# A threshold search on ScalarE: the next candidate worked out by ScalarE's own small instructions in place of GpSimd's

## The chip, the cores and the metric

The kernel runs on one core of a Trainium2 chip. The core has five engines that run at the same time, each with its own queue that is worked through strictly in order: TensorE (PE in the tables; PEld is its loading of weights), VectorE (DVE), ScalarE (ACT), GpSimd (POOL) and SyncE (SP, which issues the DMAs). They wait for each other by semaphores. The metric is the device time of one execution in microseconds (us).

## The reference

One decoder layer on 1024 tokens of width 1024, all in float32. A conditioning vector gives shift, scale and gate rows; `h = x * (1 + scale1) + shift1`; one projection gives q, k, v, the indexer's `iq`, `ik`, `iw`, and `u`. The mixer is sparse attention beside a causal pooling of `u`; then come a LayerNorm, a SwiGLU block of width 2816 and a second LayerNorm. The part that the change touches is the choice of the 256 keys that a query may attend to:

```
score = einsum('bqh,bqhs->bqs', w, relu(logits))
score = where(causal, score, -inf)
_, idx = top_k(score, 256)          # per query, of up to 1024 keys
s = softmax(q k^T over the keys in idx)
```

## The kernel before

Queries stand in eight tiles of 128, one query per partition. A query of tiles 0 and 1 has at most 256 keys, so all of them are taken. For tiles 2 to 7 the kernel looks, for every query, for the 256th largest score and turns the score row into a mask that is added in the attention (line 1058). A score is a float32 whose upper and lower 16 bits are searched one after the other, bit by bit: 15 passes over the upper half, then 16 over the lower one. A pass compares a row of 16-bit keys with a candidate per partition, counts, and moves the candidate up or down by half the last step.

Tiles 7, 6 and 5 are searched by VectorE (`search_v`). Tiles 4 and 3 together, and tile 2 alone, are two searches on ScalarE (`search_a`, line 686; `TILES_A`, line 37). Here a pass over one tile is one `Sign` activation of the keys with the negated candidate as the bias column; its accumulator adds the signs of a row into the column `cntc`. The instruction shows in the trace as ACTIVATE `junkA_T<-keys_T` (tile 4, 640 columns), `junkA_T<-keysA_X` (tile 3, 512) or `junkB_X<-keysA_X` (tile 2, 384), followed by an ACTIVATION_READ_ACCUMULATOR. Then GpSimd works out the next candidate in four instructions on columns of 1 or 2 elements per partition (lines 701 to 704; tile `colsA_X`): the sum less a limit, compared and scaled, shifted, added to the candidate. The next pass waits for them. Below, a step of the pair search is one pass over tiles 4 and 3 with its update, and a step of the single search is one pass over tile 2. There are 31 of each.

What runs around the searches: until 170 us the scores are computed (TensorE's `lg`, ScalarE's `relu_K`, VectorE's sums into `score_X`). Then come the projections of `u`, `k` and `v`: their weights are split into a high and a low part (`ws_W`; high by ScalarE, low by VectorE or GpSimd), `u` is copied to `ub_V`, summed over windows by VectorE and GpSimd, split into `phi_V` and `plo_V`, and its result leaves as `pout_K`; `k` goes to `rope_V` and `kr_K`, `v` to `vf_V`. From 395 us on the attention runs over units of one pair of heads and one query tile, tiles 7 and 6 first: the query's operands `qab_H` and `qab_W`, the scores `s`, VectorE's maximum (CUSTOM_DVE `sm_H<-s,score_X`), ScalarE's exponential, GpSimd's division, transposes `pT`, products `o`. After it come the output projection and the SwiGLU block, to 1336 us.

The order in each queue is not written out by hand. Line 154 records each instruction, estimates when its engine would reach it, and before issuing it asks `fill` (line 772) whether a step of an open search fits in front: a search says what it needs next by `yield`, an engine's letter and an estimated time. So the search steps are spread as filling between the other work by an estimate made when the program is built; on the chip the queues then run in that fixed order (`PIN`, line 39). `need(i)` (line 768) makes the attention's first use of a tile wait until its search is in the queues.

A ScalarE search has two places where VectorE takes part: after the 15th step (lines 706 to 718: the upper half is fixed, the keys are rewritten for the lower half), and after the 31st (lines 720 to 743: the mask, with a scan over the row for ties).

Of the kernel before, what the change touches and what calls it, by code (L numbers as in the profile page):

```python
# [20 lines left out]
P = 128  # L21
# [31 lines left out]
SYNC = 0.06  # L53
UPDATE = "G"
POOL_AT = 3
# [126 lines left out]
def decoder_layer_kernel(  # L182
# [458 lines left out]
    def bisect(tiles, cols, on_act):  # L641
# [23 lines left out]
        for m, i in enumerate(tiles):  # L665
# [4 lines left out]
            if on_act:  # L670
                V.tensor_scalar(one(thr, m), one(kp, m), -2.0, -float(P * (i + 1)), ALU.mult, ALU.add)
        sum_w = sum(w_(i) for i in tiles)
# [13 lines left out]
        def search_a(bits, low):  # L686

            V.memset(cand, 0.5 - float(1 << (bits - 1)))
            for b in range(bits - 1, -1, -1):
                yield "A", 1.13 * sum_w + 0.18 * nt  # L690
                for m, i in enumerate(tiles):
                    A.activation(trash(i), kv[i].bitcast(U16 if low else I16), AF.Sign, bias=one(cand, m),
                                 accum_out=one(cntc, m))
                yield UPDATE, 0.5
                half = float(1 << (b - 1)) if b > 0 else 1.0
                if UPDATE == "V":
                    V.tensor_tensor(pr, cntc, thr, ALU.is_ge)
                    V.tensor_scalar(pr, pr, -float(1 << b), half, ALU.mult, ALU.add)
                    V.tensor_tensor(cand, cand, pr, ALU.add)
                else:  # L700
                    G.tensor_tensor(pr, cntc, thr, ALU.subtract)
                    G.tensor_scalar(pr, pr, 0.0, -float(1 << b), ALU.is_ge, ALU.mult)
                    G.tensor_scalar(pr, pr, half, 0.0, ALU.add, ALU.add)
                    G.tensor_tensor(cand, cand, pr, ALU.add)
            yield "V", 0.1
            V.tensor_scalar(cand, cand, -1.0, 0.5, ALU.mult, ALU.add)

        yield from (search_a(15, False) if on_act else search_v(15, kp, False))
        V.tensor_copy(M, cand)
        for m, i in enumerate(tiles):  # L710
# [5 lines left out]
            if on_act:  # L716
                V.tensor_scalar(one(thr, m), one(ng, m), -2.0, -float(P * (i + 1)), ALU.mult, ALU.add)
        yield from (search_a(16, True) if on_act else search_v(16, ng, True))
# [53 lines left out]
    def fill(q, until):  # L772
        while True:
            todo = [st for st in streams if (st[1][0] == q.name and start(st) + st[1][1] <= until + SLACK.get(q.name, 0.0))
                    or (st[1][0] == "G" and start(st) < until)]
            if not todo:
# [1130 lines left out]
```

## Time and profile before

| | us |
|---|---|
| median of 3 runs | 1338.66 (1336.64 to 1338.84) |
| profiled execution, its own time | 1337.45 |
| its span in the trace | 1335.70 |
| PE busy in the span | 1197.2 (90%) |
| DVE busy | 1071.7 (80%) |
| POOL busy | 780.7 (58%) |
| ACT busy | 604.0 (45%) |

The span is the time from the first to the last instruction in the trace; the profiled execution's time lies 1.75 us above it, and 1.21 us below the median. The busy shares are averages over stages with different limits; the stage in which the searches run is 143 to 433 us. In a timeline row, the number in brackets at the end is how long the engine sat idle before the instruction, and behind the arrow stands what ended the wait.

### The profile page before, as it was taken

Reading aid. Unit: us, or ns where it says so; the run is one execution under the profiler, and the core shown is the slowest. Engines: PE = TensorE matmul, PEld = TensorE weight load, DVE = VectorE, ACT = ScalarE, POOL = GpSimd, SP = SyncE. Lnnn points to the kernel's source line nnn. Section 1 sums busy time; section 2 is a strip of 40 time slices with the busy share of each in tenths; the row PEclk is TensorE's granted clock in tenths of the full one; section 3 lists DMA queues with packets and bytes.
Section 4 is the critical chain, followed back from the end, with each engine's and each line's share of the span. In section 5 each row is a group of like instructions: output and inputs, shape, how many; then the busy total and the mean of one; then the engine's idle time right before and its main releaser. Section 6 shows DMA issues by size and latency. Waiting matters only on the chain.

```text
span 1335.7 us, 16132 instructions
## 1 busy us (share of the span) xinstructions
PE 1197.2 (90%) x5462; PEld 932.9 (70%) x5462; DVE 1071.7 (80%) x1769; ACT 604.0 (45%) x1149; POOL 780.7 (58%) x743
## 2 busy tenths in 40 slices
PE   7979996967768997999789999999999999999996
PEld 6646575746545664788677878878787887878775
DVE  6898889899997688566688687777768787777698
ACT  3346642653746776625644333333334243333431
POOL 1392684766434354527678484755748485666848
PEclk8989997978878998999799999999999999999998
DMA  9640030301000166430030201112120101113113
GB/s 337 232 158 17 17 95 16 111 32 48 32 24 1 33 213 223 156 119 1 24 102 27 78 32 64 36 60 67 44 79 32 64 32 64 63 36 122 39 62 122
DMA packets 34905, 103.91 MB, mean 78 GB/s; under 512 B 3843, under 2 KB 3843, under 8 KB 33286
## 3 DMA queue, kind: packets, MB, share of 16 engines
q1 hardware_dynamic: 34822, 102.88, 22.2%
q8 instruction: 43, 0.70, 0.2%
q14 instruction: 40, 0.33, 0.1%
HBM read 93.42 MB, written 9.45 MB: 77 GB/s over the span
## 4 chain that ended last, share of the span: by engine, by line
PE 38%; DVE 6%; POOL 4%; issue 2%; ACT 1%; DVEq 0%; POOLq 0%; ACTq 0%
PE gu L169 24%; PE dn L169 14%; DVE act_W L169 2%; POOL wraw_R L169 1%; DVE utmp_X L169 1%; POOL wraw_W L169 1%; DVE gtmp_V L169 1%; POOL wblk_T L169 0%; DVE wblk_T L169 0%; DVE hr_H L169 0%; POOL hr_H L169 0%; DVE res_X L169 0%; DVE stat_C L169 0%; POOL wblk_V L169 0%; DVE wblk_V L169 0%
## 5 line engine op out<-in xcount | busy, mean ns | idle before, releaser
L169 PE MATMUL gu<-hr_H,wblk_V 128*128 128x512 f32 (+1 forms) x924 | 215.2, 384 | 3.7 <-POOL wblk_V L169 1.9
L169 PE MATMUL gu<-hr_H,wblk_T 128*128 128x512 f32 (+1 forms) x924 | 215.8, 385 | 2.9 <-POOL wblk_T L169 1.9
L169 PEld LDWEIGHTS gu<-hr_H,wblk_T 128*128 128x128 f32 x924 | 170.9, 189 | 39.1 <-POOL wblk_T L169 3.6
L169 PEld LDWEIGHTS gu<-hr_H,wblk_V 128*128 128x128 f32 x924 | 170.1, 188 | 40.0 <-POOL wblk_V L169 3.6
L169 DVE TENSOR_TENSOR res_X<-res_X,dn 128x512 f32<-128x512 f32 (+1 forms) x253 | 159.0, 680 | 15.4 <-PE dn L169 15.3
L169 PE MATMUL pj<-ws_W,hT_H 128*128 128x512 f32 x456 | 123.8, 420 | 17.9 <-ACT pout_K L169 5.4
L169 POOL TENSOR_TENSOR wraw_R<-wraw_R 128x512 f32<-128x512 f32 x64 | 94.3, 1479 | 47.0 <-DVE wblk_T L169 23.7
L169 POOL TENSOR_TENSOR wraw_W<-wraw_W 128x512 f32<-128x512 f32 x60 | 86.6, 1450 | 58.0 <-DVE wblk_V L169 29.3
L169 PEld LDWEIGHTS pj<-ws_W,hT_H 128*128 128x128 f32 x456 | 88.5, 200 | 45.4 <-issue 14.8
L169 POOL TENSOR_SCALAR sm_H<-sm_H,stat_X 128x1024 f32<-128x1024 f32 (+7 forms) x64 | 58.5, 927 | 70.5 <-DVE stat_X L169 53.8
L169 PE MATMUL dn<-wblk_T,act_W 128*128 128x512 f32 x324 | 79.6, 395 | 4.8 <-DVE act_W L169 4.8
L169 PE MATMUL dn<-wblk_V,act_W 128*128 128x512 f32 x324 | 78.5, 391 | 2.9 <-DVE act_W L169 2.5
L169 DVE TENSOR_SCALAR_CACHE_REDUCE junk_X<-keysD_T,colsD_X 128x1024 int16<-128x1024 int16 (+1 forms) x64 | 78.9, 1270 | 0.8
L169 PEld LDWEIGHTS dn<-wblk_T,act_W 128*128 128x128 f32 x324 | 60.9, 189 | 19.5 <-DVE act_W L169 6.9
L169 PEld LDWEIGHTS dn<-wblk_V,act_W 128*128 128x128 f32 x324 | 60.4, 188 | 17.4 <-DVE act_W L169 4.2
L169 ACT ACTIVATE wblk_V<-wraw_R 128x512 fp32r<-128x512 f32 x56 | 35.2, 629 | 80.6 <-POOL wraw_R L169 62.2
L169 ACT ACTIVATE wblk_V<-wraw_W 128x512 fp32r<-128x512 f32 x53 | 33.1, 627 | 75.1 <-POOL wraw_W L169 56.5
L169 ACT ACTIVATE wblk_T<-wraw_W 128x512 fp32r<-128x512 f32 x56 | 35.0, 628 | 66.6 <-POOL wraw_W L169 50.2
L169 POOL TENSOR_TENSOR colsA_X<-colsA_X 128x1 f32<-128x1 f32 (+1 forms) x124 | 33.9, 283 | 48.3 <-ACT junkA_T L169 37.9
L169 ACT ACTIVATE wblk_T<-wraw_R 128x512 fp32r<-128x512 f32 x52 | 32.5, 627 | 61.0 <-POOL wraw_R L169 45.6
L169 POOL TENSOR_TENSOR ws_W<-raw_R,ws_W 128x1024 fp32r<-128x1024 f32 x11 | 29.9, 2721 | 51.3 <-ACT ws_W L169 51.3
L169 ACT ACTIVATE sm_H<-sm_H,stat_X 128x1024 f32<-128x1024 f32 (+7 forms) x64 | 49.0, 768 | 18.5 <-DVE stat_X L169 15.5
(299 smaller groups left out, 2815.4 us busy)
## 6 DMA issues: line engine op xcount, KB each, us to landing
wm_K<-in_wma_dram SPq DMA_DIRECT2D x16, 512.0 KB, 10.2
modraw_V<-in_wmc_dram SPq DMA_DIRECT2D x16, 512.0 KB, 4.5
wraw_R<-in_wg_dram SPq DMA_DIRECT2D x6, 1024.0 KB, 4.8
wraw_R<-in_wd_dram SPq DMA_DIRECT2D x12, 512.0 KB, 3.6
wraw_W<-in_wup_dram SPq DMA_DIRECT2D x12, 512.0 KB, 3.6
modraw_V<-in_wmg_dram SPq DMA_DIRECT2D x10, 512.0 KB, 3.7
wraw_R<-in_wup_dram SPq DMA_DIRECT2D x10, 512.0 KB, 3.5
wraw_W<-in_wg_dram SPq DMA_DIRECT2D x5, 1024.0 KB, 4.8
```

Source lines behind the costliest of these rows:

```text
L169: ins_ = f(*a, **k)
```

## The change

The four GpSimd instructions go. In their place ScalarE issues two small activations per tile. The number of keys in a row is even, and the limit is now such that sum plus limit is odd, so that it is never zero: `Sign(cntc + thr)` gives +1 or -1, and an `Identity` activation adds that, times half the step, to the candidate. Both read and write one column of one element per partition. The start value and the end conversion are adapted on VectorE, with the same number of instructions. The recorder's estimate for a step changes too, the wait for GpSimd goes from the search's list of needs, and `fill` no longer looks for GpSimd steps. So the order that the recorder makes comes out another way on every engine between 140 and 450 us.

```
@@ bisect
-                V.tensor_scalar(one(thr, m), one(kp, m), -2.0, -float(P * (i + 1)), ALU.mult, ALU.add)
+                V.tensor_scalar(one(thr, m), one(kp, m), 2.0, float(P * (i + 1) + 1), ALU.mult, ALU.add)
@@ search_a
-                yield "A", 1.13 * sum_w + 0.18 * nt
+                yield "A", 1.0 * sum_w + 0.65 * nt
                 for m, i in enumerate(tiles):
                     A.activation(trash(i), kv[i].bitcast(U16 if low else I16), AF.Sign, bias=one(cand, m),
                                  accum_out=one(cntc, m))
-                yield UPDATE, 0.5
-                half = float(1 << (b - 1)) if b > 0 else 1.0
...
-                    G.tensor_tensor(pr, cntc, thr, ALU.subtract)
-                    G.tensor_scalar(pr, pr, 0.0, -float(1 << b), ALU.is_ge, ALU.mult)
-                    G.tensor_scalar(pr, pr, half, 0.0, ALU.add, ALU.add)
-                    G.tensor_tensor(cand, cand, pr, ALU.add)
+
+                for m in range(nt):
+                    A.activation(one(pr, m), one(cntc, m), AF.Sign, bias=one(thr, m))
+                for m in range(nt):
+                    A.activation(one(cand, m), one(pr, m), AF.Identity, scale=-0.5 * float(1 << b), bias=one(cand, m))
             yield "V", 0.1
-            V.tensor_scalar(cand, cand, -1.0, 0.5, ALU.mult, ALU.add)
+            V.tensor_scalar(cand, cand, -1.0, None, ALU.mult)
@@ fill
-            todo = [st for st in streams if (st[1][0] == q.name and start(st) + st[1][1] <= until + SLACK.get(q.name, 0.0))
-                    or (st[1][0] == "G" and start(st) < until)]
+            todo = [st for st in streams if st[1][0] == q.name and start(st) + st[1][1] <= until + SLACK.get(q.name, 0.0)]
```

The first place is ScalarE's queue in the projection of `u`, from the first split `phi_V` on. Before, one step of each search stands in front of the result `pout_K`:

```order
L169 ACTIVATE phi_V_1245<-ub_V_1243 128x1024
L169 ACTIVATE ub_V_1244<-pj_1387 128x512
L169 ACTIVATE ub_V_1244<-pj_1435 128x512
L169 ACTIVATE junkA_T_613,colsA_X_606<-keys_T_611,colsA_X_606 128x640
L169 ACTIVATE junkA_T_613,colsA_X_606<-keysA_X_605,colsA_X_606 128x512
L169 ACTIVATE junkB_X_614,colsA_X_606<-keysA_X_605,colsA_X_606 128x384
L169 ACTIVATE pout_K_1251<-po_1553,const_C_78 128x512
L169 ACTIVATE pout_K_1251<-po_1554,const_C_78 128x512
```

Now, in the same place of ScalarE's queue, three steps of the pair search stand there (the last two of them are shown) and one of the single search:

```order
L168 ACTIVATE junkA_T_613,colsA_X_606<-keys_T_611,colsA_X_606 128x640
L168 ACTIVATE junkA_T_613,colsA_X_606<-keysA_X_605,colsA_X_606 128x512
L168 ACTIVATE colsA_X_606<-colsA_X_606 128x1 x4
L168 ACTIVATE junkA_T_613,colsA_X_606<-keys_T_611,colsA_X_606 128x640
L168 ACTIVATE junkA_T_613,colsA_X_606<-keysA_X_605,colsA_X_606 128x512
L168 ACTIVATE colsA_X_606<-colsA_X_606 128x1 x4
L168 ACTIVATE junkB_X_614,colsA_X_606<-keysA_X_605,colsA_X_606 128x384
L168 ACTIVATE colsA_X_606<-colsA_X_606 128x1 x2
L168 ACTIVATE pout_K_1235<-po_1557,const_C_78 128x512
L168 ACTIVATE pout_K_1235<-po_1558,const_C_78 128x512
```

The pair search's steps have moved forward: seven stand ahead of this first `phi_V` (before: three), and all of its first 15 steps ahead of the last `phi_V` (before: nine).

The second place is VectorE's queue at the start of the attention. Before, the end of the single search (`junkB`, 128x384) is mixed into the end of VectorE's own search, and the operands `qab_H` follow:

```order
L169 TENSOR_TENSOR junkB_X_614<-junkB_X_614,keysA_X_605 128x384
L169 SCALAR_TENSOR_TENSOR score_X_77<-keys_T_612,colsD_X_615 128x768
L169 TENSOR_SCALAR score_X_77<-junkB_X_614 128x384
L169 TENSOR_SCALAR score_X_77<-score_X_77 128x768
L169 TENSOR_TENSOR keys_T_612<-keys_T_612,score_X_77 128x768
L169 TENSOR_TENSOR junk_X_609<-junk_X_609,keys_T_612 128x768
L169 TENSOR_SCALAR score_X_77<-junk_X_609 128x768
L169 TENSOR_TENSOR qab_H_2590<-qT_2597,qab_H_2590 64x512 x2
L169 ISA sm_H_2589,stat_X_2584<-s_2681,score_X_77 128x1024
L169 ISA stat_X_2584 128x1
L169 TENSOR_TENSOR qab_W_2591<-qT_2602,qab_W_2591 64x512 x2
```

Now, on VectorE, the first part of the end of the pair search (128x640, 128x512) stands there, and the first maximum (ISA `sm_H`) comes behind both operands:

```order
L168 TENSOR_SCALAR colsA_X_606<-colsA_X_606 128x2
L168 CAST colsA_X_606<-colsA_X_606 128x2
L168 TENSOR_TENSOR colsA_X_606<-colsA_X_606 128x2 x2
L168 TENSOR_SCALAR keys_T_611<-score_X_77,colsA_X_606 128x640
L168 TENSOR_SCALAR junkA_T_613,colsA_X_606<-score_X_77,colsA_X_606 128x640
L168 TENSOR_SCALAR keysA_X_605<-score_X_77,colsA_X_606 128x512
L168 TENSOR_SCALAR colsA_X_606<-colsA_X_606 128x1
L168 TENSOR_TENSOR qab_H_2528<-qT_2535,qab_H_2528 64x512
L168 SCALAR_TENSOR_TENSOR score_X_77<-keys_T_611,colsA_X_606 128x640
L168 TENSOR_TENSOR qab_H_2528<-qT_2535,qab_H_2528 64x512
L168 TENSOR_SCALAR score_X_77<-score_X_77 128x640
L168 TENSOR_TENSOR qab_W_2529<-qT_2540,qab_W_2529 64x512 x2
```

The end of the single search has moved behind the eighth maximum, and the rest of the pair search's end between the first maxima; before, the whole of it lay behind the eighth. From 450 us on the order of every engine is the same in both kernels, and SyncE's order of DMAs is the same throughout.

## Rows read from the trace of the kernel before

**Rows 1.** Window, its us; busy us of PE, PEld, DVE, ACT, POOL; PEclk, DMA, GB/s.
```profile
143.00:395.00 252.00, 192.15 (x761) 146.51 (x759) 234.49 (x401) 133.96 (x274) 155.40 (x298) 0.88 0.14 49
...
405.00:410.00 5.00, 5.00 (x11) 2.41 (x11) 2.54 (x5) 0.88 (x3) 2.57 (x4) 0.50 0.00 0
...
420.00:425.00 5.00, 4.08 (x30) 2.45 (x31) 4.96 (x8) 2.11 (x4) 2.74 (x3) 1.00 0.01 3
...
450.00:470.00 20.00, 19.93 (x144) 13.70 (x143) 13.96 (x33) 14.21 (x32) 7.54 (x8) 1.00 0.19 57
```
**Rows 2.** Waits between 133 and 450 us: total, times, longest.
```profile
ACT junkB_X L169 <- POOL colsA_X L169: 42.8, 10, 13.4
ACT junkA_T L169 <- POOL colsA_X L169: 23.1, 14, 5.7
```
**Rows 3.** DVE in the timeline: its waits that end at another engine's search work.
```profile
161.35 2.67 DVE L169 SCALAR_TENSOR_TENSOR score_X<-relu_K,const_C,score_X 128x1024 f32<-128x1024 f32 x2 [2.36 <-ACT relu_K L169]
...
177.79 2.63 DVE L169 TENSOR_TENSOR ws_W<-raw_R,ws_W 128x1024 fp32r<-128x1024 f32 x1 [1.17 <-ACT ws_W L169]
...
250.94 1.23 DVE L169 SCALAR_TENSOR_TENSOR ub_V<-ub_V,ub_V 128x1024 f32<-128x1024 f32 x1 [2.60 <-POOL ub_V L169]
...
257.01 0.15 DVE L169 TENSOR_SCALAR colsA_X<-colsA_X 128x1 f32<-128x1 f32 x1 [1.06 <-POOL colsA_X L169]
```
**Rows 4.** The tile of the search columns: ns min/median/max, first and last start us, forms.
```profile
L169 POOL TENSOR_TENSOR colsA_X<-colsA_X x124: 183/193/1926, 144.2 to 415.7; 128x1 f32<-128x1 f32 x62, 128x2 f32<-128x2 f32 x62
L169 POOL TENSOR_SCALAR colsA_X<-colsA_X x124: 223/243/1906, 145.4 to 415.3; 128x1 f32<-128x1 f32 x62, 128x2 f32<-128x2 f32 x62
L169 ACT ACTIVATE junkB_X<-keysA_X,colsA_X x31: 598/602/627, 143.4 to 364.5; 128x384 bf16<-128x384 uint16 x16, 128x384 bf16<-128x384 int16 x15
...
L169 ACT ACTIVATE junkA_T<-keys_T,colsA_X x31: 812/828/840, 152.3 to 409.4; 128x640 bf16<-128x640 uint16 x16, 128x640 bf16<-128x640 int16 x15
```
**Rows 5.** ACT by operation and form: busy us, mean ns, idle before.
```profile
L169 ACT ACTIVATE sm_H<-sm_H,stat_X 128x128 f32<-128x128 f32 x8 | 3.1, 391 | 0.4 <-DVE stat_X L169 0.4
...
L169 ACT ACTIVATE const_C<-const_C 128x8 f32<-128x8 f32 x1 | 0.2, 210 | 0.6 <-DVE const_C L169 0.6
```
**Rows 6.** ACT in the timeline, a step of each search in turn.
```profile
359.32 0.83 ACT L169 ACTIVATE junkA_T<-keys_T,colsA_X 128x640 bf16<-128x640 uint16 x1 [0.65 <-POOL colsA_X L169]
...
361.00 0.60 ACT L169 ACTIVATE junkB_X<-keysA_X,colsA_X 128x384 bf16<-128x384 uint16 x1
...
362.35 0.83 ACT L169 ACTIVATE junkA_T<-keys_T,colsA_X 128x640 bf16<-128x640 uint16 x1 [0.66 <-POOL colsA_X L169]
```
**Rows 7.** ACT in the timeline: the first two splits of `u`.
```profile
218.91 1.06 ACT L169 ACTIVATE phi_V<-ub_V 128x1024 fp32r<-128x1024 f32 x1 [7.43 <-DVE ub_V L169]
...
231.60 1.06 ACT L169 ACTIVATE phi_V<-ub_V 128x1024 fp32r<-128x1024 f32 x1 [7.27 <-DVE ub_V L169]
```
**Rows 8.** All engines in the timeline around the start of the attention.
```profile
383.32 0.14 DVE L169 TENSOR_SCALAR colsA_X<-colsA_X 128x1 f32<-128x1 f32 x1
...
392.61 0.33 DVE L169 TENSOR_SCALAR score_X<-junkB_X 128x384 f32<-128x384 bf16 x1
...
394.90 1.40 DVE L169 TENSOR_TENSOR qab_H<-qT,qab_H 64x512 fp32r<-64x512 f32 x2
...
396.88 1.22 DVE L169 CUSTOM_DVE_ANT_0 sm_H<-s,score_X 128x1024 f32<-128x1024 f32 x1 [0.58 <-PE s L169]
...
409.40 0.83 ACT L169 ACTIVATE junkA_T<-keys_T,colsA_X 128x640 bf16<-128x640 uint16 x1 [4.12 <-POOL colsA_X L169]
...
415.89 0.17 DVE L169 TENSOR_SCALAR colsA_X<-colsA_X 128x2 f32<-128x2 f32 x1
...
418.41 0.15 DVE L169 TENSOR_SCALAR colsA_X<-colsA_X 128x1 f32<-128x1 f32 x1
...
419.62 2.32 DVE L169 TENSOR_TENSOR_SCAN score_X<-keys_T,colsA_X 128x640 bf16<-128x640 bf16 x1
```
**Rows 9.** The candidate columns of DVE's own search, 133 to 433 us: busy us, mean ns, idle.
```profile
L169 DVE TENSOR_SCALAR colsD_X<-colsD_X 128x3 f32<-128x3 f32 (+3 forms) x41 | 12.9, 322 | 1.1
```

More of the change, by code (lines that the diff above doesn't have):

```diff
@@ L53 @@
 SYNC = 0.06
-UPDATE = "G"
 POOL_AT = 3
@@ L693, in search_a @@
                                  accum_out=one(cntc, m))
-                yield UPDATE, 0.5
-                half = float(1 << (b - 1)) if b > 0 else 1.0
[L696 to L700, printed above, removed]
-                    G.tensor_tensor(pr, cntc, thr, ALU.subtract)
-                    G.tensor_scalar(pr, pr, 0.0, -float(1 << b), ALU.is_ge, ALU.mult)
-                    G.tensor_scalar(pr, pr, half, 0.0, ALU.add, ALU.add)
-                    G.tensor_tensor(cand, cand, pr, ALU.add)
+                for m in range(nt):
+                    A.activation(one(pr, m), one(cntc, m), AF.Sign, bias=one(thr, m))
+                for m in range(nt):
+                    A.activation(one(cand, m), one(pr, m), AF.Identity, scale=-0.5 * float(1 << b), bias=one(cand, m))
             yield "V", 0.1
-            V.tensor_scalar(cand, cand, -1.0, 0.5, ALU.mult, ALU.add)
+            V.tensor_scalar(cand, cand, -1.0, None, ALU.mult)
         yield from (search_a(15, False) if on_act else search_v(15, kp, False))
@@ L716, in bisect @@
             if on_act:
-                V.tensor_scalar(one(thr, m), one(ng, m), -2.0, -float(P * (i + 1)), ALU.mult, ALU.add)
+                V.tensor_scalar(one(thr, m), one(ng, m), 2.0, float(P * (i + 1) + 1), ALU.mult, ALU.add)
         yield from (search_a(16, True) if on_act else search_v(16, ng, True))
```

## The prediction

> **What bounds the kernel now.** I read the busy times by window first, then the waits, then the search's own tile, then the timeline of ScalarE and VectorE stretch by stretch. From 143 to 395 us VectorE is busy 234.49 of 252 us, ScalarE 133.96, GpSimd 155.40, TensorE 192.15 [rows 1]: this stage ends when VectorE is through with its own search of tiles 7, 6 and 5, since the attention begins with those tiles. So what ScalarE or GpSimd save counts here only where VectorE stands and waits for them. At the start of the attention TensorE is full at a granted clock of 0.50, which is its lower level of 1.2 GHz (405 to 410 us, 5.00 of 5); then VectorE is the full one (420 to 425: 4.96, TensorE 4.08); from 450 us TensorE is (19.93 of 20) [rows 1]. All later work is in the same order in both kernels, so that what is gained or lost by 450 us is handed on to the end.
>
> ScalarE's searches spend much time on GpSimd's answer: 42.8 and 23.1 us of idle ScalarE, 65.9 in all [rows 2]. Where the two searches alternate, a step of both takes 362.35 - 359.32 = 3.03 us, of which ScalarE works 1.68 (359.32 to 361.00) on the pair step and about 0.7 on the single step, and waits 0.66 [rows 6].
>
> **The change part by part.** *Removed from GpSimd:* 248 column instructions at 0.19 and 0.24 us in the median [rows 4], some 54 us of an engine that does not bound; with them go ScalarE's 65.9 us of waits, which did not bound either, except where VectorE stood behind them. Those places: 2.36 us at 161.35 (a `relu_K` stood behind a search step that waited for GpSimd), 1.17 at 177.79 (the `ws_W` copy, likewise), 2.60 at 250.94 (GpSimd's own `ub_V` work stood behind column instructions), 1.06 at 257.01 (the single search's 15th candidate itself) [rows 3]. Sum 7.2 us that VectorE gets back, if nothing new is late there.
>
> *Added to ScalarE:* 31 x 4 + 31 x 2 = 186 activations of one column. The trace of before has none, so I bound them: 0.21 us is the shortest activation in it (8 columns, no bias column), 0.39 one of 128 columns with a bias column [rows 5]. The search's own activations grow from 602 ns at 384 columns to 828 at 640 [rows 4], 0.88 ns a column, and so leave 0.26 us for an instruction without columns; with a bias column as here, I take 0.28. The Trainium skill, page "ScalarE: Activation LUTs", section "What ACT_TABLE_LOAD costs", states about 280 ns and 0.83 ns per column for an activation with one such operand; by that the sum stays what it is. They depend on each other: in a single step the sum, its sign and the new candidate come one after the other, so 0.5 (activation) + 0.2 (accumulator) + 2 x 0.31 = 1.34 us, against about 0.62 of ScalarE's time before; in a pair step the two tiles overlap, 1.68 + 4 x 0.19 = 2.45 (bounds 2.4, and 3.0 if each waits for the one ahead). A step of both then takes 3.8 us where it took 3.03: the chain through GpSimd was the shorter one as long as the other search filled the wait. ScalarE's own work rises by 31 x (0.77 + 0.72) = 46 us; it has 118 us free from 143 to 395 [rows 1], 66 of which were the waits. So it holds on the whole; the question is single places, since the steps were moved forward.
>
> *The projection of `u`.* ScalarE waited 7.43 and 7.27 us for VectorE ahead of the first two splits, which stand 12.7 us apart [rows 7]. Seven pair steps now stand ahead of the first split, four more than before; with its copies they are done about 12 us early. Between the first two splits ScalarE now has 3 x 2.45 + 1.34 + 4.0 of copies = 12.7 us at most: just in time. From the second to the third, two steps of each search stand in both kernels, now 3.0 us dearer, less some 1.7 of waits for GpSimd: 1.3 us late, and VectorE's next `ub_V` sum, which had no room, waits those 1.3. Behind it on VectorE stand its own search passes, so this is a true loss: -1.3. GpSimd's sums of `ub_V` come earlier and hide nothing new.
>
> *The pair search's middle on VectorE* moves up from 324 to about 259 us, in place of the single search's. ScalarE's 15th step is done at 218.9 + 8 x 2.45 + 3 x 1.34 + 11.8 of copies = 254.3 (in times of before): 5 us ahead. No wait.
>
> *The start of the attention.* Out of VectorE's way to `qab_H` goes the end of the single search, 13 instructions from 383.32 to 392.61, some 3.0 us between the others. In come eight instructions of the pair search's end, 415.89 to 418.41 and on, 2.6 us; a scan of 640 columns, 2.32 us with GpSimd at work beside it [rows 8], I take 1.5 alone; 0.3 for a compare; and `qab_W`'s two, 1.4, which stood behind the first maximum. Together +2.8; the first maximum waited 0.58 for TensorE [rows 8], which then no longer shows: it comes 2.2 us later against VectorE's search. ScalarE is no hindrance: its 31st pair step now stands ahead of `qab_H`, and by the same sum ends some 10 us ahead of VectorE. What comes back: the third unit's exponential, which stood 4.12 us behind a search step and GpSimd's answer [rows 8], does not any more, and VectorE's rest of the pair search falls into the time when TensorE is full at half clock and VectorE has 2.5 of 5 us free, instead of the time when VectorE is full and TensorE has 18% free. That 18% over the 20 us to 435 bounds the return at 3.7; I take 2.5. Net +0.3.
>
> Sum: -7.2 + 1.3 + 2.2 - 2.5 = -6.2 us, on the profiled 1337.45 as on the median 1338.66, since it is a difference: **1332.5 us**. With the bounds (pair step at 3.0: another 3 us lost in the projection; return at 0 or 3.7; half of the 7.2 not found) it lies between -10 and +1.
>
> **The rivals.** *A: a wait for ScalarE takes the place of the waits for GpSimd (slower).* If a pair step costs more than 3.1 us, the 15th step is later than VectorE's middle: 5 us of room over 8 steps. At 3.4, VectorE waits 2.4 there, and by the same 0.95 a step 3 x 0.95 + 2 x 0.95 = 4.7 more for the splits of `u`; with 1.3 and 2.2, and without any return, that is 10.6 lost for 7.2 found: 1342. For it: the longer step of both, 3.8 against 3.03, and that the recorder's estimate counts less than that. Against: rows 5 put the small activation at 0.39 at most, and with it the step at 3.1 hardly. The Trainium skill speaks for this rival: the page "ScalarE: Activation LUTs", section "Rules for kernel authors", gives adds and multiplies to VectorE and not to ScalarE. Here VectorE is the full engine, so a gain by that rule is not to be had in this stage.
>
> *B: no change.* The gain before 395 is smaller (VectorE and TensorE fall back on each other at 161 us, where scores come 3.4 us apart whatever ScalarE does, and only 4 of the 7.2 remain), and the first maximum's 2.2 us are not returned since TensorE is full at half clock just then: 4 - 1.3 - 2.2 = 0.5 faster, 1338.
>
> *C: more than 10 us faster.* VectorE's column instructions in its own search take 0.32 us in the mean [rows 9], where 0.17 is what such a one takes undisturbed [rows 8]: 41 x 0.15 = 6 us in which something held them up, and GpSimd's column instructions take up to 1.9 us where the median is 0.19 [rows 4]. If GpSimd's columns are the cause, all of it comes back on the full engine: 1332.5 - 6 = 1326.5. The Trainium skill, page "SBUF — State Buffer", section "SBUF: two separate sides", has the two engines share a port pair as an exclusive lock. Against it: the lengthened ones lie beside GpSimd's long instructions, which stay; one of 0.2 us can hold up another by 0.2 at most.
>
> *D: the change does not do what it says* would show as more table loads on ScalarE; the order has four in both kernels. No chance given.
>
> **How the numbers follow.** This kernel's measurement tells 0.2%, 2.7 us, from no change. Forecast (1327 to 1336) 0.58; C 0.08; B 0.20; A 0.14. So faster 0.66, same 0.20, slower 0.14. The range reaches into B and A on one side and to C on the other: 1326.5 to 1340.
>
> **What would show it.** ScalarE's 186 activations `colsA_X<-colsA_X` at 0.26 to 0.30 us; ScalarE busy about 50 us more, GpSimd 70 less; VectorE's waits of 2.36, 1.17, 2.60 and 1.06 gone, a wait of 1 to 2 us for ScalarE at the third `ub_V` sum, none in the pair search's middle; `gr_G`, then the first maximum, some 6 and some 4 us earlier than before; 450 us of before reached at 444. I am wrong if VectorE's row shows waits of several us for `colsA_X` or `ub_V` from ScalarE, or if the first maximum comes later than 396.9.

## The result, and the profile after

The change makes the kernel faster by 0.6%: a median of 1330.57 us (1327.57 to 1333.88, 6 runs) against 1338.75 (1336.64 to 1340.93, 6 runs), ratio 0.994, 95% interval 0.9919 to 0.996. A second set (e12 below) gave 1329.43 against 1338.74, ratio 0.9933 (0.992 to 0.9947). That is 8.2 to 9.3 us gained, 6.2 forecast. The profiled execution, the quickest of its six, took 1327.57 us with a span of 1325.8, 9.9 less than the profiled one of before.

First the same windows as in [rows 1], of the kernel after (columns as there). ScalarE is busier by 40 us from 143 to 395, GpSimd less by 69; from 405 to 410 us TensorE's clock is already on its way up (0.63, it was 0.50), and from 420 to 425 TensorE is full and VectorE is not, where it was the other way round.

```profile
143.00:395.00 252.00, 188.11 (x768) 144.07 (x766) 240.63 (x409) 173.61 (x458) 86.24 (x59) 0.88 0.14 49
405.00:410.00 5.00, 5.00 (x25) 4.29 (x24) 3.85 (x7) 4.06 (x12) 2.00 (x2) 0.63 0.00 0
420.00:425.00 5.00, 5.00 (x38) 4.07 (x36) 4.02 (x9) 3.19 (x7) 2.21 (x2) 1.00 0.00 0
450.00:470.00 20.00, 19.90 (x135) 12.85 (x133) 15.61 (x37) 14.24 (x32) 8.37 (x7) 1.00 0.45 146
```

The search columns on ScalarE after (columns as in [rows 4]); it now waits for no answer of GpSimd, and the 65.9 us of [rows 2] are gone:

```profile
L168 ACT ACTIVATE colsA_X<-colsA_X x186: 277/280/300, 144.8 to 409.2; 128x1 f32<-128x1 f32 x186
```

VectorE's waits between 133 and 450 us after, some of them (total, times, longest). The four of [rows 3] answer to the last four lines: 2.36 has become at most 1.1, 1.17 at most 0.2, 2.60 is 0.3, and a wait for `colsA_X` is no longer listed.

```profile
DVE sm_H L168 <- PE s L168: 5.0, 8, 1.0
...
DVE score_X L168 <- ACT relu_K L168: 2.0, 3, 1.1
...
DVE ub_V L168 <- ACT ub_V L168: 0.5, 1, 0.5
DVE ws_W L168 <- ACT ws_W L168: 0.5, 2, 0.2
DVE ub_V L168 <- POOL ub_V L168: 0.3, 1, 0.3
```

Where the time came from is read best from two marks on VectorE: its scan of tile 7, which ends its own search, and the 13th maximum of the attention. First before (these rows were not shown above; the first maximum is in [rows 8]), then after:

```profile
378.16 2.35 DVE L169 TENSOR_TENSOR_SCAN score_X<-keysD_T,colsD_X 128x1024 bf16<-128x1024 bf16 x1
...
422.61 1.20 DVE L169 CUSTOM_DVE_ANT_0 sm_H<-s,score_X 128x1024 f32<-128x1024 f32 x1
430.42 1.08 DVE L169 CUSTOM_DVE_ANT_0 sm_H<-s,score_X 128x896 f32<-128x896 f32 x1
...
435.44 1.22 DVE L169 CUSTOM_DVE_ANT_0 sm_H<-s,score_X 128x1024 f32<-128x1024 f32 x1 [1.18 <-PE s L169]
```

```profile
373.60 2.35 DVE L168 TENSOR_TENSOR_SCAN score_X<-keysD_T,colsD_X 128x1024 bf16<-128x1024 bf16 x1
...
394.66 1.23 DVE L168 CUSTOM_DVE_ANT_0 sm_H<-s,score_X 128x1024 f32<-128x1024 f32 x1
...
416.77 1.21 DVE L168 CUSTOM_DVE_ANT_0 sm_H<-s,score_X 128x1024 f32<-128x1024 f32 x1
422.42 1.09 DVE L168 CUSTOM_DVE_ANT_0 sm_H<-s,score_X 128x896 f32<-128x896 f32 x1 [0.83 <-PE s L168]
...
426.13 1.23 DVE L168 CUSTOM_DVE_ANT_0 sm_H<-s,score_X 128x1024 f32<-128x1024 f32 x1
```

The scan comes 4.56 us earlier, the 13th maximum 9.31: 4.75 us are won behind the scan. Up to it the search itself wins more than the 4.56: this execution reached the first instruction of VectorE's search (`keysA_X`) 0.62 us later than the one of before (142.27 against 141.65 us), so 5.18 us are won from there to the scan. Yet the first maximum, counted from the scan, comes later (21.06 us against 18.72). The gap from the 10th to the 11th maximum, 7.81 us before, is 5.65.

### The profile page after: what moved, and what is told of

It is laid out like the page before. It is cut to its first block, busy times and chain, and to the rows that moved or that the text cites. A ratio compares the mean times of both kernels' runs of the same rounds, so it can differ in the third digit from the quotient of the medians.

```text
span 1325.8 us, 16034 instructions
## 1 busy us (share of the span) xinstructions
PE 1186.7 (90%) x5462; PEld 927.9 (70%) x5462; DVE 1070.5 (81%) x1769; ACT 642.7 (48%) x1335; POOL 709.2 (53%) x495
## 4 chain that ended last, share of the span: by engine, by line
PE 37%; DVE 6%; POOL 4%; issue 2%; ACT 1%; DVEq 0%; POOLq 0%; ACTq 0%
PE gu L168 23%; PE dn L168 14%; DVE act_W L168 2%; POOL wraw_R L168 2%; DVE utmp_X L168 1%; POOL wraw_W L168 1%; DVE gtmp_V L168 1%; POOL wblk_V L168 1%; POOL wblk_T L168 0%; DVE wblk_T L168 0%; DVE hr_H L168 0%; POOL hr_H L168 0%; DVE wblk_V L168 0%; DVE res_X L168 0%; DVE stat_C L168 0%
## 5 line engine op out<-in xcount | busy, mean ns | idle before, releaser
L168 POOL TENSOR_TENSOR wraw_W<-wraw_W 128x512 f32<-128x512 f32 x60 | 86.7, 1452 | 57.9 <-DVE wblk_V L168 29.3
L168 PEld LDWEIGHTS dn<-wblk_V,act_W 128*128 128x128 f32 x324 | 60.4, 188 | 17.4 <-DVE act_W L168 4.2
L168 ACT ACTIVATE wblk_V<-wraw_W 128x512 fp32r<-128x512 f32 x53 | 33.1, 628 | 75.0 <-POOL wraw_W L168 56.4
L168 ACT ACTIVATE wblk_T<-wraw_W 128x512 fp32r<-128x512 f32 x56 | 35.0, 628 | 65.9 <-POOL wraw_W L168 50.2
L168 POOL TENSOR_TENSOR ptmp_C<-rope_V,gr_G 128x512 f32<-128x512 f32 x16 | 25.8, 1610 | 66.1 <-ACT rope_V L168 65.7
```

The source lines that it names most:

```text
L168: ins_ = f(*a, **k)
```

## The experiments

All times are medians; differences of one or two us are near what the measurement can tell. From the profiled execution of each kernel this table gives the start of the scan of tile 7, three maxima counted from it, and from when TensorE's granted clock is 1.00 (to about 1 us, from windows of 1 us). A profile is a single execution: the one of after is the quickest of its set, the one of e6 the slowest, so the marks say less about the medians than about the order of events.

| kernel | median us | scan | 1st max. | 10th | 13th | clock 1.00 from |
|---|---|---|---|---|---|---|
| before | 1338.7 | 378.2 | +18.7 | +44.5 | +57.3 | 414 |
| after | 1330.6, 1329.4 | 373.6 | +21.1 | +43.2 | +52.5 | 409 |
| e1 GpSimd columns added | 1330.6 | 375.3 | +21.1 | +43.2 | +52.6 | 411 |
| e2 ScalarE's candidates, old places | 1343.4 | 380.0 | +20.2 | +47.8 | +61.2 | 418 to 424, then 432 |
| e3 GpSimd's candidates, new places | 1345.7 | 387.5 | +22.2 | +43.3 | +53.4 | 425 |
| e4 pair's end later | 1336.6 | 373.5 | +21.0 | +47.0 | +61.3 | 426 |
| e5 before, no pair's end | 1334.8 | 378.5 | +18.7 | +41.8 | +54.3 | 415 |
| e6 after, no pair's end | 1330.4 | 373.9 | +17.4 | +43.5 | +57.9 | 423 |
| e7 filler | 1330.9 | 376.9 | +21.1 | +44.6 | +54.0 | 401 to 414, then 418 |
| e8 longer steps | 1333.0 | 377.2 | +20.7 | +40.8 | +52.7 | 411 |
| e9 e6 with filler | 1328.5 | 375.6 | +16.6 | +40.2 | +51.8 | 402 |
| e10 end later, with filler | 1328.5 | 375.7 | +18.3 | +41.2 | +52.1 | 399 |
| e11 old estimate | 1332.9 | 386.6 | +10.9 | +33.1 | +43.9 | 415 |

**e1, GpSimd's column instructions given back.** `emit` issues an instruction past the recorder, so that nothing else moves.

```
+            G.emit("memset", cols[:, 40:56], 0.0)
...
+                for q_ in (10, 11, 10, 11):
+                    G.emit("tensor_scalar", col(q_), col(q_ + 2), 1.0, 0.0, ALU.add, ALU.add)
```

> The changed kernel, every engine's order untouched, with four GpSimd column instructions given back to each of the 62 search steps, on spare columns that nobody reads; ScalarE still works out its own candidates. They are not paced by the steps: GpSimd runs them as soon as its order allows. Theory (the gain is VectorE's waits for a search step, and the place of the pair search's end): nobody waits for them, so 0 to 2.6 us at most over the changed kernel's 1330.6, the 2.6 if GpSimd's ub_V sums stand behind them again: 1331 to 1333. Rival C (column instructions of GpSimd hold VectorE up, 6 us): 1336 to 1337, and VectorE's colsD TENSOR_SCALAR up from 299 ns toward 322.

Measured 1330.59 us (ratio 0.9939, 0.992 to 0.9958): nothing. GpSimd has its 248 column instructions again (busy 761 us, 709 after), and VectorE's own column instructions take no longer for it (mean 299 ns after). The group of [rows 9] (12.9 us, mean 322 ns), in e1:

```profile
L168 DVE TENSOR_SCALAR colsD_X<-colsD_X 128x3 f32<-128x3 f32 (+3 forms) x41 | 11.6, 291 | 1.1
```

Rival C is out at its size of 6 us. At one place e1's profile has the columns in VectorE's way: four of them (1.70 us at 172.94) stand ahead of GpSimd's `score_X`, for which VectorE then waits 0.87 us instead of 0.18. The median shows no cost.

**e2 and e3, the mechanism without the places, and the places without the mechanism.** In e2 ScalarE works out its candidates, and the recorder counts as before, GpSimd steps included; in e3 the reverse (`plan` counts an instruction without issuing it).

```
@@ e2: the changed kernel with
-                yield "A", 1.0 * sum_w + 0.65 * nt
+                yield "A", 1.13 * sum_w + 0.18 * nt
...
+                yield "G", 0.5
+                G.plan("tensor_tensor", pr, cntc, thr)
...
-                    A.activation(one(pr, m), one(cntc, m), AF.Sign, bias=one(thr, m))
+                    A.emit("activation", one(pr, m), one(cntc, m), AF.Sign, bias=one(thr, m))
@@ e3: the changed kernel with
-                    A.activation(one(pr, m), one(cntc, m), AF.Sign, bias=one(thr, m))
+                    A.plan("activation", one(pr, m), one(cntc, m), bias=one(thr, m))
...
+                G.emit("tensor_tensor", pr, cntc, thr, ALU.subtract)
...
+                G.emit("tensor_tensor", cand, cand, pr, ALU.add)
```

> ScalarE's own candidates, as in the changed kernel, but with the recorder's old costs and its old GpSimd steps counted as if they were there, so that the steps stand where they stood before: the single search's end ahead of the first maximum, the pair search's end between the 8th and the 11th maximum. Theory (the change's gain has two parts: waits taken out of VectorE's way up to its search's end, 4.6 us, and the pair search's end moved out of the stretch where VectorE is full, about 4.4 net): the first part comes, the second doesn't: 1333.5 to 1335, first maximum some 4 to 5 us earlier than before's 396.9, and all of it still there but no more at the 13th. Rival (the return at the attention's start comes from the exponential that no longer stands behind a search step): 1331 or less, since that wait goes here too. Rival (the order alone): 1338.

> The other way round: GpSimd's four column instructions work out the candidate as before, but the steps stand where the changed kernel has them as far as the recorder decides. Theory: ScalarE's steps, now back to back, each wait for GpSimd's answer (a pair step 3.0 instead of 2.4 us), so VectorE meets late steps at the u projection and in the searches' middle, 3 to 10 us in all, while some 4 us of the attention's start are kept: 1334 to 1342, with ScalarE's waits for colsA_X above the 65.9 us of before. Rival (the order alone makes the gain, the GpSimd chain is harmless): 1331. Rival C says nothing of its own here.

Measured: e2 1343.36 us (1.0034, 1.0022 to 1.0045), e3 1345.68 (1.0055, 1.0034 to 1.0075). Both are slower than before, e2 by 4.8 us and e3 by 7.2; for e2 the theory and both rivals were wrong, and e3 lies above the 1342 that was expected at most. The stretch from the first instruction of VectorE's search to the scan, in before, after, e2 and e3 (window, its us; busy us of VectorE; PEclk, DMA, GB/s):

```profile
141.65:378.16 236.51, 219.07 (x376) 0.89 0.15 51
142.27:373.60 231.33, 220.41 (x376) 0.90 0.15 52
144.43:380.00 235.57, 222.47 (x374) 0.91 0.15 51
142.01:387.50 245.49, 218.84 (x374) 0.89 0.15 51
```

So e2 is not slower up to the scan: counted from there it wins 0.9 us, where the changed kernel wins 5.2; that its scan stands later in the table comes from an execution that was 2.8 us late before the searches began, with nothing changed in the order up to there. Whether its other executions were late too is not known. VectorE stands idle less than before (13.1 us; 17.4 before, 10.9 after), and it takes longer over the same work (3.4 us more; 1.3 after). Part of the latter is plain in the timeline of e2: twice an instruction of VectorE runs beside GpSimd's `ws_W`. The first ends 1.08 us behind it, the second with it; before, they took 1.22 and 0.17 us, with no `ws_W` of GpSimd beside them.

```profile
241.05 3.14 POOL L168 TENSOR_TENSOR ws_W<-raw_R,ws_W 128x1024 fp32r<-128x1024 f32 x1 [1.78 <-ACT ws_W L168]
...
241.86 3.41 DVE L168 SCALAR_TENSOR_TENSOR ub_V<-ub_V,ub_V 128x1024 f32<-128x1024 f32 x1
...
248.55 2.36 POOL L168 TENSOR_TENSOR ws_W<-raw_R,ws_W 128x1024 fp32r<-128x1024 f32 x1 [4.36 <-ACT ws_W L168]
...
248.69 2.25 DVE L168 TENSOR_SCALAR colsD_X<-colsD_X 128x3 f32<-128x3 f32 x1
```

In this execution e2 loses its time behind the scan: its 13th maximum comes 3.9 us later than before's (+61.2 against +57.3). There its order is not the one of before: on VectorE the single search's end stands as a block ahead of `qab_H`, on TensorE eight scores (four before) stand ahead of the first transposes, and the clock falls back to 0.50 from 424 to 432 us. So e2 says little of the change's places behind the scan; which of these three makes the loss was not separated.

e3 has ScalarE's waits for GpSimd back, 86.1 us instead of the 65.9 of [rows 2], since the steps follow each other more closely; from the search's first instruction to the scan it loses 9.0 us against before. The time up to the scan thus needs the mechanism and the places together: in these executions the one alone wins 0.9 us, the other alone loses 9.0, and both together win 5.2. Behind the scan e3 is nearly as quick as after (13th maximum +53.4 against +52.5), with the pair search's end around the first maxima as after; but its order is not quite the changed kernel's (the single search's end stands there too), so that the places make the start of the attention is likely and not shown. Waits of ScalarE in e3 between 133 and 400 us:

```profile
ACT junkB_X L168 <- POOL colsA_X L168: 49.8, 12, 11.6
ACT junkA_T L168 <- POOL colsA_X L168: 36.3, 15, 8.6
```

**e11, one line put back:** the estimate of a step alone.

```
-                yield "A", 1.0 * sum_w + 0.65 * nt
+                yield "A", 1.13 * sum_w + 0.18 * nt
```

> The changed kernel with one line put back: the recorder again counts a search step on ScalarE at 1.13 per 1024 columns and 0.18 per tile (a pair step 1.63, a single one 0.60), where the step takes 2.40 and 1.26. Theory (the gain needs steps that stand where they fit; e2 and e3 showed that mechanism and places are worth nothing apart): steps stand too densely among the relus and the splits of u, VectorE waits for ScalarE there, and its own search, pushed back by the recorder, ends later: 1336 to 1346. Rival (the mechanism alone makes the gain): 1330 to 1332.

Measured 1332.89 us (0.9955, 0.9938 to 0.9971): 2.3 to 3.5 us above the changed kernel by the medians, with intervals that overlap; it lies between the theory (1336 to 1346) and the rival (1330 to 1332). The waits for `relu_K` that the theory named are there (7 of them, 12.5 us in all, 2.0 after), though not by the places alone: TensorE's granted clock from 140 to 160 us was 0.83 in this execution and 1.00 in the one of after, and e7, with the changed kernel's places and the same 0.83, has 6.4 us of them. The recorder also takes the whole pair search, end included, ahead of VectorE's scan, and much of what is lost up to there comes back behind it (+43.9).

```profile
DVE score_X L168 <- ACT relu_K L168: 12.5, 7, 2.5
```

**e8, longer steps.**

```
+                for m in range(2 * nt):
+                    A.emit("activation", one(cols[:, 40:44], m % 4), one(pr, 0), AF.Identity)
```

> The changed kernel with twice as many small activations again behind every search step of ScalarE (4 more in a pair step, 2 more in a single step, on spare columns that nobody reads), issued past the recorder: a pair step of about 3.2 us instead of 2.4, a single one of 1.7 instead of 1.26, some 37 us more of ScalarE. Theory as forecast (ScalarE holds on the whole, single places don't; a pair step above 3.1 us is later than VectorE's middle): 3 to 7 us slower than the changed kernel, 1333.5 to 1337.5, with VectorE's waits for relu_K, ub_V and colsA_X from ScalarE back. Rival (ScalarE is far off the path): 1330 to 1332. Rival A at full size: 1341 or more.

Measured 1333.04 us (0.9962, 0.9949 to 0.9974), 2.5 to 3.6 above the changed kernel by the medians, a little under the 1333.5 expected; its interval still touches that of the first set and not that of the second. The additions overlap, and a pair step grew to 2.78 us only (starts at 192.39 and 195.17), a single one to 1.44 (1.26 to 1.38 after); so the point of rival A, 3.1, was not reached. ScalarE is near the path all the same: VectorE's `plo_V` waits for ScalarE's `phi_V` 3 times here, 3.5 us in all (2.2 after). How much of the loss is ScalarE's is open, since the clock from 140 to 160 us was 0.91 in this execution and 1.00 in the one of after.

**e4, the end of the pair search held back.** These steps of VectorE ("W") are taken only when four units of the attention are out, or when their mask is needed.

```
-            yield "V", 1.7 * w_(i) + 0.1
+            yield ("W" if i in (4, 3) else "V"), 1.7 * w_(i) + 0.1
```

> The changed kernel with only the end of the pair search (the masks of tiles 4 and 3, from the second compare on) held back by the recorder until four units of the attention are out: most of it then stands between the 6th and the 11th maximum. Theory: the first maximum comes 1.5 to 2.3 us earlier against VectorE's search, but the return of about 6.8 us up to the 13th maximum is mostly lost, since this work now stands where VectorE is the full engine: 1332.5 to 1335.5. Rival (the return comes from ScalarE's wait that is gone, not from the place): 1328 to 1330, the first maximum's 2 us being kept.

Measured 1336.58 us (0.9975, 0.9961 to 0.9989), 5 to 7 us lost against the changed kernel, a little more than the theory gave. The way is another one: the first maximum did not move (+21.0), and VectorE is not the full engine. TensorE is, at half clock until 426. Its order changed too: as before the change, four scores `s<-qab_W` stand ahead of the first transposes. Windows of e4, columns as in [rows 1]:

```profile
405.00:415.00 10.00, 10.00 (x32) 6.71 (x31) 6.41 (x16) 6.67 (x15) 4.55 (x5) 0.50 0.00 0
415.00:425.00 10.00, 10.00 (x32) 5.82 (x33) 8.39 (x19) 4.10 (x7) 3.26 (x3) 0.50 0.01 2
```

**e5 and e6, the end of the pair search left out.** The masks of tiles 4 and 3 are left out in both.

```
+            if i in (4, 3):
+                biased.add(i)
+                continue
```

> The kernel before without the masks of tiles 4 and 3 (the 16 VectorE instructions that end the pair search are left out, so these two tiles are masked by their raw scores). They take some 10 us of VectorE and stand between the 8th and the 11th maximum. Theory (the place of these instructions is what returns: VectorE is the full engine there): 5 to 8 us fall away, 1331 to 1334, and the gap from the 10th to the 11th maximum falls from 7.8 us to under 5. Rival (the return is the third exponential that no longer waits for GpSimd, and the clock that rises sooner with it): that wait is still here, so at most 3 us: 1335.5 to 1338.5.

> The changed kernel without the same 16 instructions (the masks of tiles 4 and 3 left out), which stand there around the first eight maxima, half of them ahead of the first. Theory: what they cost here is their delay of the first maximum, 2.4 us, and little else: 1327 to 1329, so that with e5 the change loses most of its advantage at this place. Rival (place is nothing, the instructions cost the same in both): 5 to 8 us less, 1323 to 1326.

Measured: e5 1334.8 us (0.9971, 0.9962 to 0.998), 3.4 less than before; e6 1330.37 (0.9946, 0.9934 to 0.9958), nothing less than after. Neither theory was met: e5 lies between the theory (1331 to 1334) and the rival (1335.5 to 1338.5), its gap from the 10th to the 11th maximum fell to 7.02 us only (under 5 expected), and e6 lies above both its ranges. The 16 instructions cost 3.4 us at their old place, and leaving them out at the new one won nothing. In e5 VectorE is free (4.87 of 10 us), and TensorE is full instead:

```profile
415.00:425.00 10.00, 9.01 (x52) 5.43 (x53) 4.87 (x14) 6.41 (x12) 6.42 (x11) 1.00 0.01 2
425.00:435.00 10.00, 10.00 (x79) 7.25 (x77) 6.12 (x11) 8.41 (x16) 2.95 (x3) 1.00 0.08 27
```

In e6 the first maximum comes 3.6 us sooner after the scan, and this wins nothing. In its profile, of the slowest of its runs, TensorE is full at half clock to about 423 us, 14 us longer than after. But e6 is no clean comparison: as in e4, TensorE's order changed with the instructions left out, and four scores stand ahead of the first transposes again.

```profile
395.00:405.00 10.00, 10.00 (x23) 5.22 (x24) 4.60 (x9) 6.96 (x18) 2.21 (x2) 0.50 0.00 0
405.00:415.00 10.00, 10.00 (x30) 6.33 (x29) 3.04 (x7) 4.47 (x10) 4.21 (x4) 0.50 0.00 0
415.00:425.00 10.00, 10.00 (x48) 6.16 (x47) 7.41 (x20) 4.09 (x7) 4.59 (x4) 0.61 0.01 2
```

```profile
401.44 2.16 PE L168 MATMUL s<-kr_K,qab_W 128*128 128x512 f32 x4
403.53 3.67 PE L168 MATMUL pT<-const_C,sm_H 128*128 128x128 f32 x16
```

**e7, e9 and e10, TensorE kept busy.** The 90 fillers stand in TensorE's gaps from 375 us on; e9 adds them to e6, e10 to the changed kernel with the pair's end held back by one unit (as e4, with 1 in place of 4; nothing is left out there).

```
+    filler = psA("filler")
+    for _ in range(90):
+        T.emit("transpose", filler[:, 0:P], ident, ident)
```

> The changed kernel with 90 TensorE transposes of the identity, which nobody reads, in TensorE's gaps ahead of and between the first scores of the attention; every order but TensorE's is untouched. In the changed kernel TensorE stands from 379.5 to 390.7 us, and then works at a granted clock of 0.50 until 408.3, 12 us of it without a gap. Theory (the half clock at the start prices everything up to the 8th maximum; the changed kernel's lead grows from 2.2 to 8.0 us there partly because its clock rises 5.2 us sooner): if the fillers bring the clock up by 397 instead of 408.3, 2 to 4 us are won, 1326.5 to 1328.5; if they don't, they only stand in the way of the first scores by 2 to 4 us, 1332.5 to 1335. Rival (VectorE alone sets the pace there): no change but for that, 1330 to 1332, whatever the clock.

> e6 (the changed kernel without the masks of tiles 4 and 3) with the 90 filler transposes of e7 on TensorE. New theory after e6 and e7: at the attention's start two limits take turns, TensorE at half clock and VectorE with the pair search's end; e6 took away the second alone and e7 the first alone, and neither moved the end. With both away the 13th maximum comes 4 us or more sooner against VectorE's scan of tile 7 than the 52.5 us of the changed kernel, if the clock rises by 402: 1324 to 1327.5. Rival (neither limit is what holds the attention's start, or the half clock only comes back later): 1329.5 or more.

> A version that keeps all of the computation: the changed kernel with the pair search's end held back until one unit of the attention is out, and the 90 fillers on TensorE. By the same theory the first four maxima come up to 3 us sooner, the clock rises by 402, and the end of the search falls between the 4th and the 10th maximum, where VectorE has most of its free time: 1326 to 1330 if the clock then holds; 1331 to 1335 if it falls back to 0.50 between 410 and 425 as in e7. Rival (only VectorE's sum of work counts): 1330 to 1331.

Measured: e7 1330.94 us (0.9948, 0.9936 to 0.996), e9 1328.49 (0.9921, 0.9906 to 0.9937), e10 1328.5 (0.9923, 0.9907 to 0.9939). In e7 the clock is up 8 us sooner and wins nothing, as its rival had it: VectorE is the full engine then (9.31 of 10), TensorE has 2 us without work, and the clock falls back to 0.50 between 414 and 418.

```profile
405.00:415.00 10.00, 7.98 (x47) 5.49 (x46) 9.31 (x20) 7.63 (x20) 4.31 (x5) 0.98 0.00 0
415.00:425.00 10.00, 10.00 (x63) 6.48 (x62) 7.88 (x22) 6.50 (x14) 4.34 (x4) 0.85 0.01 2
```

With both limits away (e9) the 13th maximum comes 0.8 us sooner after the scan (+51.8), not 4, and the median is between the theory (1327.5 at most) and the rival (1329.5 at least): the theory of two limits in turn is not borne out. What sets the pace then was not found. e10 computes everything and is the fastest of the complete kernels, but by 0.9 to 2.1 us against the two sets of the changed kernel, with intervals that overlap: no gain is shown.

**e12, the changed kernel again.**

> The changed kernel once more, nothing edited, since its first six runs lie in two groups (1327.6 to 1328.8 and 1332.3 to 1333.9) and e1, e6, e7 and e10 are read against it. Theory (the two groups are executions in which TensorE's clock does or does not dip while the scores of tile 7 are worked out, as the 0.94 to 0.97 of e1 between 130 and 170 us against 1.00 in the first profile): a median of 1329 to 1332, with both groups seen again. If it comes at 1328.5 or less, e10 is no gain.

Measured 1329.43 us (1327.8 to 1332.19). Of all 11 runs of the changed kernel seven lie from 1327.6 to 1329.8 and four from 1332.2 to 1333.9. In the profiles, where the clock between 150 and 170 us is 1.00 (after, e4, e6, e12) the scan stands at 372.9 to 373.9; where it is lower (0.97 in e1, 0.87 in e7, 0.94 in e9 and e10) it stands at 375.3 to 376.9, with nearly the same order of work up to there. That this makes the two groups is not shown. e1's execution had the dip and took 1329.5 us; e6's had none and took 1333.3. No profile was taken of the four slower runs, but the granted clock of whole executions is known: 0.952 to 0.955 in the seven quicker ones, 0.947, 0.947, 0.948 and 0.954 in the four slower. By an estimate from these profiles, a dip as in e7 (0.87 over 20 us) lowers this mean by 0.002, and a rise of the clock that comes 14 us later, as in e6, by 0.005. So for three of the four a late rise at the attention's start is the likelier cause; it stays open.

## Why the prediction was right, and which of its steps were not

The time came out as forecast (1330.6 in 1327 to 1336, and at 8.2 a little more than the 6.2), and most single marks did: ScalarE's small activations at 0.28 us, a pair step of 2.40 (2.45 forecast) and a single one of 1.26 to 1.38 (1.34, though its terms add up to 1.32), GpSimd's 70 us less, no wait in the middle of the pair search, no table load more. Other marks missed: ScalarE is busier by 39 us (46 to 50), the third `ub_V` sum waits 0.50 us for ScalarE (1 to 2), the first maximum comes 2.2 us earlier (4), and 450 us of before is reached at about 440 to 441 (444). The size of the gain is right partly by luck, since errors of opposite sign cancel.

*VectorE gets back 7.2 us, less 1.3 in the projection: 5.9 up to its search's end.* Measured 5.18 from the search's first instruction to the scan, by another sum: VectorE stands idle 6.5 us less (10.9 against 17.4) and is busy 1.3 us more, so the forecast's 1.3 of waiting came as 1.3 of longer instructions. The first two waits, taken by the clock of the trace, gave 3.33 of their 3.53 (the first `ub_V` sum starts at 200.63 before, at 197.30 after). The other two gave 1.23 of 3.66. The wait of 2.60 was not only a matter of column instructions, as the forecast read it: GpSimd's own `ws_W`, 2.38 us long, stood last ahead of its `ub_V` sum. Timeline of before:

```profile
248.35 2.38 POOL L169 TENSOR_TENSOR ws_W<-raw_R,ws_W 128x1024 fp32r<-128x1024 f32 x1
250.70 0.21 POOL L169 TENSOR_TENSOR ub_V<-ub_V,const_C 128x16 f32<-128x16 f32 x1
```

And the forecast had ScalarE 1.3 us late at the third `ub_V` sum; it was late by 0.50, but the sum itself, moved forward, now runs beside that `ws_W` and takes 2.85 us where it took 1.22 (timeline of after):

```profile
243.56 2.69 POOL L168 TENSOR_TENSOR ws_W<-raw_R,ws_W 128x1024 fp32r<-128x1024 f32 x1 [3.52 <-ACT ws_W L168]
...
244.47 2.85 DVE L168 TENSOR_TENSOR ub_V<-ub_V 128x1024 f32<-128x1024 f32 x1 [0.50 <-ACT ub_V L168]
...
247.66 1.23 DVE L168 SCALAR_TENSOR_TENSOR ub_V<-ub_V,ub_V 128x1024 f32<-128x1024 f32 x1 [0.34 <-POOL ub_V L168]
```

0.50 + 1.63 + 0.34 = 2.47 off 3.66 leaves 1.19. The Trainium skill, page "SBUF — State Buffer", section "SBUF: two separate sides", has one instruction of VectorE with two SBUF inputs and one of GpSimd that reads SBUF lock each other out of a shared port pair for its whole length. These rows agree: VectorE's sum ends 1.07 us behind the end of GpSimd's `ws_W` (247.32 against 246.25), and alone it takes 1.22. The lock was weighed for the short column instructions (rival C), where e1 shows no cost in the median, and not looked for in the long ones.

The reason, too, was too simple: it counted the waits that go as a gain that is there by itself. e2 shows that it is not: with the waits for GpSimd gone and the steps counted as before it wins 0.9 us up to the scan, not 5.2. There VectorE waits 4.6 us for `relu_K` up to 200 us (3.9 before, 2.0 after), and its instructions meet GpSimd's `ws_W` twice.

*"It comes 2.2 us later against VectorE's search"*, counted as 2.2 us lost: this step of the sum failed. The first maximum does come 2.34 later, but the transposes behind it do not. TensorE in the timeline before, then after:

```profile
398.26 2.13 PE L169 MATMUL s<-kr_K,qab_W 128*128 128x512 f32 x4 [0.69 <-DVE stat_X L169]
400.85 2.13 PE L169 MATMUL s<-kr_K,qab_W 128*128 128x512 f32 x4 [0.45 <-DVE stat_X L169]
402.90 4.67 PE L169 MATMUL s<-kr_K,qab_H 128*128 128x512 f32 x8
407.50 2.16 PE L169 MATMUL s<-kr_K,qab_W 128*128 128x512 f32 x4
409.59 3.67 PE L169 MATMUL pT<-const_C,sm_H 128*128 128x128 f32 x16
412.92 1.70 PE L169 MATMUL s<-kr_K,qab_W 128*128 128x512 f32 x4
```

```profile
396.04 4.21 PE L168 MATMUL s<-kr_K,qab_W 128*128 128x512 f32 x8 [1.92 <-DVE stat_X L168]
400.18 4.67 PE L168 MATMUL s<-kr_K,qab_H 128*128 128x512 f32 x8
404.78 3.67 PE L168 MATMUL pT<-const_C,sm_H 128*128 128x128 f32 x16
408.11 1.93 PE L168 MATMUL s<-kr_K,qab_W 128*128 128x512 f32 x8
```

Counted from the scan, the first transposes start at 31.18 us instead of 31.43. Between the first maximum and them 2.59 us are made good: 0.45 is the gap that TensorE had ahead of its second four scores, and some 2.1 are four `s<-qab_W` scores that stood ahead of the transposes at half clock. They have not gone: the changed order of TensorE puts them behind the transposes (eight there, four before). No run separates this new order of TensorE from the place of the pair search's end, and in e4 and e6 both changed together. That the lateness costs nothing is what the marks of this pair show; why is argued from the rows above.

*The return of 2.5 us (bound 3.7).* The place was right, and e5 prices VectorE's 16 instructions there at 3.4 us. From the start of the first transposes to 0.2 us ahead of the 13th maximum, before and after (columns as in [rows 1]):

```profile
409.59:435.23 25.64, 21.80 (x126) 15.01 (x125) 21.02 (x43) 16.98 (x33) 10.66 (x12) 0.91 0.02 2
404.78:425.92 21.14, 20.43 (x130) 14.93 (x129) 17.32 (x41) 15.13 (x34) 8.60 (x8) 0.91 0.03 7
```

The stretch is 4.50 us shorter. TensorE stands idle in it for 0.71 us instead of 3.84, so 3.13 of the 4.50 are work that it no longer waits for; the other 1.37 are TensorE's own busy time, of which an earlier rise of the clock (3.9 us behind the start of the transposes, 4.4 before) explains some 0.2 by an estimate (half of the 0.46 us, since the clock was half). The rest is open, as is the part of the forecast that lay on the exponential's wait of 4.12 us: no run separated it.

In sum: 5.9 forecast and 5.18 measured up to the scan; 0.3 forecast and 4.75 measured behind it, and 2.2 of that difference is the lateness that did not last. Both numbers are from single executions, and the one of after is a quick one: 9.9 us apart where the medians are 8.2 to 9.3. Behind the 13th maximum the lead hardly moves (9.31 us there, 9.9 at the span's end), as the forecast had it.

## What to carry to other kernels

When a step is moved from one engine to another, its estimate in whatever places the work belongs to the change. Here the new mechanism, placed by the old count, won 0.9 of the 5.2 us up to the scan and came out 4.8 us slower in all; the old mechanism at the new places came out 7.2 slower; both together won 8 to 9. Where instructions move, look what the long additions of GpSimd now run beside. Before a later start is counted as a loss, look at the order behind it: what stood between the start and the next step, and where that stands now. That two engines took turns as the limit at the attention's start (VectorE by its work, TensorE by its half clock) was argued from e6 and e7; with both relieved only 0.8 us were won (e9), so it is not shown.

## What the hardware showed that was not expected

- Small activations overlap: each takes 280 ns, but four of a pair step take 0.83 us together and the two of a single step, which wait for each other, 0.62.
- TensorE's clock rose to 1.00 at the first unit's 16 transposes in before, after, e1, e2, e3, e5 and e12, or less than 2 us behind them. In e4 the same block ran from 407 to 410 us and the clock stayed at 0.50 until 426, in e6 it ran from 403.5 to 407 and the clock stayed there until 423, with TensorE full all the time in both. Why it stayed there is open; part of e4's loss hangs on it.
- An instruction of VectorE beside a long addition of GpSimd can take far longer: a 128x1024 sum 2.85 us (after) and 3.41 (e2) instead of 1.22, and a 128x3 column instruction 2.25 instead of 0.17 (e2), each ending with GpSimd's or about 1.1 us behind it. The 248 one-column instructions of GpSimd in e1 cost nothing in the median; its profile shows them in VectorE's way once, for 0.7 us.
